# The low half of the weight split, on VectorE in place of GpSimd, in a hybrid decoder layer

## The chip, the cores and the metric

One core of one Trainium2 chip runs the whole program. The metric is the device time of one execution in microseconds (us). Engines are named as the profile names them: PE is TensorE, ACT is ScalarE, DVE is VectorE, POOL is GpSimd, SP is the engine that issues most transfers.

## What is computed

One layer over 512 tokens of width 1024, all in float32. Three token mixers run side by side on one combined projection, are gated and summed, and a feed-forward follows (from the reference, cut):

```
h = rms_norm(x, norm1_g)
u = h @ w_in
y_a = dsa_mixer(...)   # 16 heads; an index picks the 128 keys that count
y_b = nsa_mixer(...)   # 16 heads; compressed blocks, chosen blocks, window
y_c = ssd_mixer(...)   # Mamba-2, chunks of 128 tokens, 32 heads
mix = gates[0]*(y_a @ w_br_dsa) + gates[1]*(y_b @ w_br_nsa) + gates[2]*(y_c @ w_br_ssd)
x = x + mix @ w_out
h = rms_norm(x, norm2_g)
x = x + square(relu(h @ w_ff1)) @ w_ff2
```

## The kernel before, in words

**Split products.** A float32 operand is written as hi + lo, both in a faster float32 format (F32R). A large product is then three matmuls: hi with hi, hi with lo, lo with hi (`mm3`, L317 to L319). The weights are split as they arrive. `WS.load` (L130) sends 128x1024 weights from memory into one of three `wraw` buffers by SP. `WS.split` (L141) makes `whi`, a rounding copy on ScalarE (L150), and `wlo`, the subtraction `wraw - whi` (L151); each has six buffers. `tick` keeps the splits up to three pieces ahead of the products, and `free` gives the buffers back once the last product that reads them is issued. There are 212 pieces in a run.

**Two streams.** `filler` (L543 on) yields all large products: projections of `h`, then the branch products (`branches`, L1200), `w_out` and the feed-forward (`ff_up`, L1338, `ff_down`, L1367). `main` yields what comes between: the DSA index (L709), DSA attention, the SSD (L1071), NSA attention. The loop at the end takes steps from both in turn by estimated costs. Main's instructions have a higher priority. A scheduler of the framework then sets the order on each engine by priority and by its own reckoning of when an operand is ready; each engine works through its order strictly. So a change of one instruction's engine can move instructions on every engine.

**Attention** (`pipeline`, L820) takes a unit of 4 heads and 128 queries: scores on TensorE (L755, L756), mask and maximum on VectorE (L757), exponential on ScalarE (L764), scaling of `p` on VectorE for three heads (L777) and on GpSimd for the fourth (L775), transposes on TensorE (L791), hi and lo of the transposed `p` on ScalarE and VectorE (L795, L796), products with V (L803, L804; L943 for the compressed branch), the sum `yt` (L810, L811), written to memory as rows of y and read back as `yr` (L664) for the branch products.

**SSD** (`stage2`, L1094 on): VectorE makes `E` from the cumulated decays (eight L1102 for a chunk and group, then L1110) and `cbm` (L1100); GpSimd scales `xs` three times (L1105, L1108, L1112) and the state (L1132); TensorE multiplies (L1098, L1121, L1127, L1137). Beside it runs the convolution of the filler, on VectorE (L684).

**Branch products and feed-forward.** `branches` takes a0, a1, c0, c1, b0, b1 in order; b1 can't begin until the last NSA rows are back from memory. In `ff_up` ScalarE applies relu (L1362), VectorE squares (L1363), ScalarE rounds (L1364), VectorE takes the low half (L1365).

Of the kernel before, what the change touches and what calls it, by code (L numbers as in the profile page):

```python
# [10 lines left out]
ALU = mybir.AluOpType  # L11
# [25 lines left out]
def build_kernel(ctx, tc, A, out):  # L37
    nc = tc.nc
    pe, act, dve, pool = nc.tensor, nc.scalar, nc.vector, nc.gpsimd
    done = set()  # L40

    def dram(ap, off, dims):
        return bass.AP(tensor=ap.tensor, offset=ap.offset + off, ap=dims)

    def bc(ap, shape):
        return ap.to_broadcast(shape)

    def f(ap):
        return ap.bitcast(F32)
# [3 lines left out]
    def popen(name, side="left", space=None, bufs=1):  # L53
        kw = dict(name=name, bufs=bufs, side=side)
        if space is not None:
            kw["space"] = space
            kw.pop("side")
        cm = tc.tile_pool(**kw)
        p = cm.__enter__()
        open_pools[name] = cm  # L60
        return p
# [17 lines left out]
    yc_d = scratch("yc_d", [2048, S])  # L79
    rs_d = scratch("rs_d", [4, 128])  # L80

    # ------------------------------------------------------------------ constants
    cp = popen("const")
    psp = ctx.enter_context(tc.tile_pool(name="psp", bufs=1, space=PSUM))

# [31 lines left out]
    g1b = x0.tile([128, D], F32, name="g1b")  # L117
    act.dma_start(g1b, dram(A["norm1_g"], 0, [[0, 128], [1, D]]))

    # ------------------------------------------------------------------ weights  # L120
    class WS:
        def __init__(s):
            s.specs, s.raw, s.hl = [], {}, {}
# [17 lines left out]
        def split(s):  # L141
            i = s.nsplit
            while s.nload <= i:
                s.load()
            _, n, w = s.specs[i]
            r = s.raw.pop(i)
            m = n * w
            hi = wp.tile([128, 1024], F32R, name="whi", tag="whi", bufs=NS)
            lo = wp.tile([128, 1024], F32R, name="wlo", tag="wlo", bufs=NS)
            act.activation(hi[:, :m], r[:, :m], AF.Copy)  # L150
            pool.tensor_tensor(lo[:, :m], r[:, :m], f(hi[:, :m]), op=ALU.subtract)  # L151
            s.hl[i] = (hi[:, :m].rearrange("p (a b) -> p a b", b=w), lo[:, :m].rearrange("p (a b) -> p a b", b=w))
            s.nsplit += 1

# [70 lines left out]
            ff1[q + 1] = plan_ff1(q + 1)  # L225
        ff2[q] = plan_ff2(q)

    # first weights run ahead of the activations
    for t in range(1, NB):
        ws.load()  # L230
        nc.sync.dma_start(xt[t], dram(A["x"], t * 128 * D, [[D, 128], [1, D]]))

    # ------------------------------------------------------------------ small constants
    def bcast_load(name, ap, n, pl):
        t = pl.tile([128, n], F32, name=name)
        nc.sync.dma_start(t, dram(ap, 0, [[0, 128], [1, n]]))
        return t
# [24 lines left out]
                           pattern=pat or [[step, n]], channel_multiplier=chm)  # L262
        return t

    # ------------------------------------------------------------------ x -> h^T
    sq_junk = x0.tile([128, D], mybir.dt.bfloat16, name="sq_junk")
    ss1 = cp.tile([128, NB], F32, name="ss1")
    rs1 = cp.tile([128, NB], F32, name="rs1")
# [18 lines left out]
    for i, b in enumerate((2, 3)):  # L287
        for half in range(2):
            cur = 2 * b + half
            r = slice(64 * half, 64 * half + 64)  # L290
# [21 lines left out]
    dve.tensor_copy(pos2[64:128], pv_[:, :, :, 1])  # L312
    pclose("x0")

    # ------------------------------------------------------------------ matmul helpers
    def mm3(o, lh, ll, rh, rl, first, last):
        pe.matmul(o, lh, rh, start=first, stop=False)  # L317
        pe.matmul(o, lh, rl, start=False, stop=False)  # L318
        pe.matmul(o, ll, rh, start=False, stop=last)  # L319
# [43 lines left out]
    hh = lambda k: hTh[:, k, :]  # L363
    hl = lambda k: hTl[:, k, :]

    # ------------------------------------------------------------------ persistent attention operands
    def r_tile(pl, name, shape):
        return pl.tile(shape, F32R, name=name)

# [5 lines left out]
    kc = r_tile(kv, "kc", [128, 2, 2, 32])  # L375
# [74 lines left out]

    RB, AB, TB, EB, TG = [int(v) for v in "33222"]

    # ------------------------------------------------------------------ filler: all large products
    def q_block(o, plan):
        ss = stg.tile([128, NB, 8], F32, name="ssq", bufs=2)

# [25 lines left out]


    def cmp_prep(u1, e1):
        """k_cmp and v_cmp operands from the raw kc, vc columns."""
        for v in range(2):
            xc = e1.tile([128, 16, 2, 32], F32, name="xc", bufs=1)
            wh = []
            for i in range(2):
                w_ = e1.tile([128, 8, 64], F32, name="cmpw", tag="cw", bufs=2)  # L490
                nc.sync.dma_start(w_, dram(A["nsa_cmp_w"], v * 131072 + i * 65536, [[64, 128], [8192, 8], [1, 64]]))
                wh.append(w_)
            pool.memset(xc[:, :, :, 31:32], 0.0)
            p = ps("pT", [128, S])
            for t in range(NB):
                pe.transpose(p[:, t * 128:t * 128 + 128], u1[:, t, v * 128:v * 128 + 128], ident)
            yield 440
            for g in range(2):
                for half in range(2):
                    r = slice(64 * half, 64 * half + 64)  # L500
                    base = p[64 * g:64 * g + 64, half:half + 1]
                    win = bass.AP(tensor=base.tensor, offset=base.offset, ap=[base.ap[0], [2, 16], [16, 31]])
                    dve.tensor_tensor(xc[r, :, g, :31], win, bc(pos2[r, v, :, None], [64, 16, 31]), op=ALU.add)
            yield 440
            pc = ps("pT", [128, 512])
            for a in range(16):
                pe.matmul(pc[:64, :64], xc[:, a].rearrange("p g n -> p (g n)"), wh[a // 8][:, a % 8], start=a == 0, stop=a == 15)
            if v == 0:
                kx = e1.tile([64, 64], F32, name="kx")
                dve.tensor_copy(kx, pc[:64, :64])  # L510
                yield 1800
                rt = rms_rows(e1, kx[:, None, :], 64, 1, 1.0 / 64, EPS)
                dve.scalar_tensor_tensor(kx, kx, rt[:64, 0:1], g_nsa[:64, 0, :], op0=ALU.mult, op1=ALU.mult)
                kcs = e1.tile([64, 2, 2, 64], F32R, name="kcs")
                kxb = bc(kx[:, None, :], [64, 2, 64])
                act.activation(kcs[:, 0], kxb, AF.Copy)
                dve.tensor_tensor(kcs[:, 1], kxb, f(kcs[:, 0]), op=ALU.subtract)
                for i in range(2):
                    pk = ps("pT", [128, 64], F32R)
                    pe.transpose(pk, kcs[:, i].rearrange("p a b -> p (a b)"), identr[:64, :64])  # L520
                    act.activation(kc[:, :, i], f(pk).rearrange("p (g n) -> p g n", g=2), AF.Copy)
                yield 600
            else:
                vx = e1.tile([64, 64], F32, name="vx")
                dve.tensor_copy(vx, pc[:64, :64])
                yield 1800
                sel = e1.tile([64, 2, 4, 32], F32, name="sel")
                dve.tensor_copy(sel, bc(ident[:64, 0:64].rearrange("p (g n) -> p g n", g=2)[:, :, None, :], [64, 2, 4, 32]))
                zero = e1.tile([128, 256], F32, name="zero")
                pool.memset(zero, 0.0)  # L530
                vzf = vz.rearrange("p a b c d -> p (a b c d)")
                for z in range(2):
                    act.activation(vzf[:, 256 * z:256 * z + 256], zero, AF.Copy)
                for g in range(2):
                    pk = ps("pT", [128, 64])
                    pe.matmul(pk, sel[:, g].rearrange("p a b -> p (a b)"), vx, start=True, stop=True)
                    for h in range(4):
                        r = slice(32 * h, 32 * h + 32)
                        act.activation(vz[r, g, h % 2, 0], pk[r], AF.Copy)
                        dve.tensor_tensor(vz[r, g, h % 2, 1], pk[r], f(vz[r, g, h % 2, 0]), op=ALU.subtract)  # L540
                    yield 300
# [130 lines left out]

    ypools = {}

    # ------------------------------------------------------------------ conv + silu of the SSD inputs
    def conv(m, p):
        cw = lambda k: convc[:, k * 24 + m:k * 24 + m + 1]
        raw = stg.tile([128, S], F32, name="craw", tag="r", bufs=RB)
# [23 lines left out]
                nc.sync.dma_start(dst.rearrange("(t p) c -> p t c", p=128), ev)  # L702
            defer(1, tr)

    # ------------------------------------------------------------------ DSA index and its top 128
    MASK = {}
    RIDX = R0

# [27 lines left out]
        pclose("idx")  # L736
        return sv

    # ------------------------------------------------------------------ attention units
    class U:  # L740
        pass

# [120 lines left out]
            u.prep = lambda i=i: prep(i)  # L863
        return us

    # ------------------------------------------------------------------ NSA
    SM = {}
    PC = {}
    CT = {}

    def cmp_a(b, g, q2, ratio):
        """Compressed-branch softmax of 8 heads and the block choice."""
        s_ = ps("sc", [128, 512])
        sv = s_.rearrange("p (h i n) -> p h i n", i=2, n=32)
        for h in range(8):
# [136 lines left out]
                    us.append(u)  # L1012
        return us

    # ------------------------------------------------------------------ SSD
    def ssd_prelude():
        n = [128, 128]
        pre = [gp.tile([128, 4, 128], F32, name="pre", tag="gt", bufs=TG) for _ in range(2)]
# [177 lines left out]
        a = t[r0:r0 + n, :]  # L1196
        return bass.AP(tensor=a.tensor, offset=a.offset, ap=[[0, 128]] + [list(e) for e in a.ap])

    # ------------------------------------------------------------------ branches, merge, w_out, feed-forward
    def branches(ya):  # L1200
        bp = popen("br")
        mix = bp.tile([128, KT, S], F32, name="mixf")
# [89 lines left out]
        pclose("yC")  # L1292
        pclose("yB")
        pclose("br")
        # w_out + residual + norm2
        fp = popen("ff")
        x2 = fp.tile([128, NB, D], F32, name="x2")
        h2h = fp.tile([128, KT, S], F32R, name="h2h")
# [82 lines left out]
        pclose("ffl")  # L1381
        pclose("ff")

    # ------------------------------------------------------------------ the two streams and their merge
    def main():
        nonlocal at
        HI[0] = 0
# [32 lines left out]
    while True:  # L1420
        with tc.high_priority(offset=HI[0]):
            r = next(mg, None)
# [42 lines left out]
```

## Time and profile before

| | |
|---|---|
| runs, median (lowest to highest of 3) | 1495.65 us (1494.98 to 1497.01) |
| profiled execution, first to last instruction | 1496.3 us |
| PE busy | 1400.1 us |
| DVE busy | 1013.8 us |
| POOL busy | 715.6 us |
| ACT busy | 691.0 us |

The profiled execution is one of the program's runs, taken with a hardware profiler; its span stands for its own time and lies within the three runs shown. A row of a group of instructions reads: line, engine, operation, what it writes and reads, shape, how often; then busy time, mean duration in ns, and the engine's idle time just before them with what ended it. A duration runs from the start of an instruction to its end, with any time in which it is held after it has started. Matmul records overlap, so their mean is longer than the distance between them.

### The profile page before, as it was taken

The page shows a single profiled execution, that of the slowest core. Times are in us where ns is not written, and L with a number is a line of the kernel's source. Part 1 is how long each engine was busy: PE and PEld are TensorE (multiplying, and loading weights), DVE is VectorE, ACT ScalarE, POOL GpSimd, SP SyncE. Part 2 cuts the span into 40 slices and gives each one's busy share as a digit, 9 for nine tenths or more (in the row PEclk, how much of TensorE's full clock was granted, in tenths as well). Part 3 has the DMA queues.
Part 4 walks back from the last instruction along what each step waited for, and adds up shares of the span by engine and source line. Part 5 has one row for each costly group of instructions (what it writes and reads, how often), then busy time and mean ns, then how long its engine had stood idle before and what let it go on. Part 6 is the DMA issues. An engine that isn't in the chain of part 4 may idle for free.

```text
span 1496.3 us, 19760 instructions
## 1 busy us (share of the span) xinstructions
PE 1400.1 (94%) x6832; PEld 1149.9 (77%) x6832; DVE 1013.8 (68%) x1887; ACT 691.0 (46%) x1364; POOL 715.6 (48%) x456
## 2 busy tenths in 40 slices
PE   6998999899988898899999999999999999999999
PEld 5886788677866676787788877777678888888887
DVE  4699956789789987757767898786645751433411
ACT  4545445667644454545555555545333441422220
POOL 5544534434245366544334765644753542544351
PEclk9999999999999998999999999999999999999999
DMA  5323464443565565654324744422652322323231
GB/s 194 99 77 106 150 203 130 125 122 94 139 198 173 166 199 159 200 170 130 106 89 147 206 140 117 117 78 78 211 201 82 113 99 71 127 73 112 83 106 50
DMA packets 218272, 195.92 MB, mean 131 GB/s; under 512 B 15664, under 2 KB 165564, under 8 KB 218172
## 3 DMA queue, kind: packets, MB, share of 16 engines
q1 hardware_dynamic: 212700, 183.12, 41.3%
q0 software_dynamic: 4608, 8.39, 2.0%
q10 hardware_dynamic: 864, 3.15, 0.5%
q8 instruction: 54, 0.88, 0.2%
q14 instruction: 46, 0.38, 0.1%
HBM read 157.85 MB, written 36.77 MB: 130 GB/s over the span
## 4 chain that ended last, share of the span: by engine, by line
PE 56%; DVE 29%; ACT 5%; DMA 5%; issue 4%; POOL 2%; SPq 0%; DVEq 0%; ACTq 0%; POOLq 0%
PE pj L318 15%; PE pj L319 15%; PE pj L317 15%; DVE E L1102 3%; DVE cacc L684 3%; DVE p L777 3%; ACT p L764 3%; DVE ptl L796 2%; DVE mask L731 2%; DVE m L730 1%; DVE p L757 1%; PE pT L791 1%; PE sc L1137 1%; PE sc L755 1%; DMA wraw<-in_w_in_dram 1%
## 5 line engine op out<-in xcount | busy, mean ns | idle before, releaser
L151 POOL TENSOR_TENSOR wlo<-wraw,whi 128x1024 fp32r<-128x1024 f32 (+3 forms) x212 | 479.0, 2269 | 416.7 <-ACT whi L150 394.9
L150 ACT ACTIVATE whi<-wraw 128x1024 fp32r<-128x1024 f32 (+3 forms) x212 | 207.3, 982 | 210.9 <-PE pj L319 102.1
L319 PE MATMUL pj<-hTh,wlo 128*128 128x512 f32 x384 | 156.8, 408 | 0.0
L317 PE MATMUL pj<-hTh,whi 128*128 128x512 f32 x384 | 155.4, 405 | 0.1
L318 PE MATMUL pj<-hTl,whi 128*128 128x512 f32 x384 | 154.8, 403 | 0.0
L764 ACT ACTIVATE p<-p,nb,rs 128x256 f32<-128x256 f32 (+3 forms) x192 | 123.3, 644 | 59.2 <-DVE nb L762 58.9
L317 PE MATMUL pj<-whi,hTh 128*128 128x512 f32 (+2 forms) x352 | 138.7, 396 | 8.1 <-DVE zo L575 2.2
L318 PE MATMUL pj<-wlo,hTh 128*128 128x512 f32 (+2 forms) x352 | 138.7, 395 | 0.8 <-POOL wlo L151 0.8
L319 PE MATMUL pj<-whi,hTl 128*128 128x512 f32 (+2 forms) x352 | 139.0, 396 | 0.0
L1363 DVE TENSOR_TENSOR fr<-fr 128x512 f32<-128x512 f32 x32 | 80.8, 2530 | 56.2 <-ACT fr L1362 56.2
L1371 DVE TENSOR_TENSOR x<-x,pj 128x512 f32<-128x512 f32 x32 | 22.0, 687 | 138.3 <-PE pj L319 137.8
L777 DVE TENSOR_SCALAR p<-p,rc 128x256 f32<-128x256 f32 (+3 forms) x144 | 113.3, 837 | 1.1
L775 POOL TENSOR_TENSOR p<-p,rc 128x256 f32<-128x256 f32 (+3 forms) x48 | 37.9, 790 | 152.5 <-DVE rc L770 51.8
L317 PE MATMUL pj<-yh,whi 128*128 128x512 f32 x256 | 103.4, 406 | 5.1 <-DVE gld L1282 3.1
L318 PE MATMUL pj<-yl,whi 128*128 128x512 f32 x256 | 103.6, 405 | 0.2 <-DVE yl L666 0.2
L319 PE MATMUL pj<-yh,wlo 128*128 128x512 f32 x256 | 103.0, 402 | 0.0
L318 PE MATMUL pj<-wlo,fh 128*128 128x512 f32 x256 | 99.6, 389 | 0.0
L319 PE MATMUL pj<-whi,fo 128*128 128x512 f32 x256 | 99.6, 389 | 0.0
L317 PE MATMUL pj<-whi,fh 128*128 128x512 f32 x256 | 98.8, 389 | 0.0
L319 PE MATMUL pj<-h2h,wlo 128*128 128x512 f32 (+1 forms) x256 | 96.2, 376 | 0.0
L318 PE MATMUL pj<-h2l,whi 128*128 128x512 f32 (+1 forms) x256 | 96.2, 376 | 0.0
L317 PE MATMUL pj<-h2h,whi 128*128 128x512 f32 (+1 forms) x256 | 96.1, 376 | 0.0
(333 smaller groups left out, 3322.5 us busy)
## 6 DMA issues: line engine op xcount, KB each, us to landing
wraw<-in_w_in_dram SPq DMA_DIRECT2D x84, 512.0 KB, 4.1
wraw<-in_w_ff_dram SPq DMA_DIRECT2D x64, 512.0 KB, 4.0
gld<-g_d SPq DMA_DIRECT2D x48, 256.0 KB, 3.1
q_d<-qev SPq DMA_DIRECT2D x32, 256.0 KB, 2.3
qu<-q_d POOLq DMA_DIRECT2D x32, 256.0 KB, 4.2
E<-ac_d SPq DMA_DIRECT2D x16, 512.0 KB, 4.3
wraw<-in_w_br_ssd_dram SPq DMA_DIRECT2D x16, 512.0 KB, 4.2
g_d<-gth SPq DMA_DIRECT2D x24, 256.0 KB, 2.0
```

Source lines behind the costliest of these rows:

```text
L150: act.activation(hi[:, :m], r[:, :m], AF.Copy)
L151: pool.tensor_tensor(lo[:, :m], r[:, :m], f(hi[:, :m]), op=ALU.subtract)
L317: pe.matmul(o, lh, rh, start=first, stop=False)
L318: pe.matmul(o, lh, rl, start=False, stop=False)
L319: pe.matmul(o, ll, rh, start=False, stop=last)
L684: dve.scalar_tensor_tensor(acc[:, sh:], raw[:, :S - sh], cw(k), acc[:, sh:], op0=ALU.mult, op1=ALU.add)
L731: dve.match_replace(wk, m8, wk, TAKEN)
L764: act.activation(u.p[h][:, :n], u.p[h][:, :n], AF.Exp, bias=u.nb[:, h:h + 1], scale=rs8[:, u.b, u.h0 + h:u.h0 + h + 1], accum_out=u.sm[:, ...
L775: pool.tensor_tensor(u.p[h][:, :n], u.p[h][:, :n], bc(rc[:, h:h + 1], [128, n]), op=ALU.mult)
L777: dve.tensor_scalar(u.p[h][:, :n], u.p[h][:, :n], rc[:, h:h + 1], None, op0=ALU.mult)
L1102: dve.tensor_scalar(u.E[:, h], u.E[:, h], col(sv["acm"], c, g)[:, h:h + 1], 0.0, op0=ALU.subtract, op1=ALU.min)
L1363: dve.tensor_tensor(r, r, r, op=ALU.mult)
```

## The change

One line. The subtraction that makes the low half of a weight piece is issued on VectorE.

```
@@ def split(s)
             act.activation(hi[:, :m], r[:, :m], AF.Copy)
-            pool.tensor_tensor(lo[:, :m], r[:, :m], f(hi[:, :m]), op=ALU.subtract)
+            dve.tensor_tensor(lo[:, :m], r[:, :m], f(hi[:, :m]), op=ALU.subtract)
```

The rest of the diff takes out comments. The scheduler's order changes on every engine. Two places:

VectorE, where the SSD begins. `E` and `cbm` belong to the SSD, `cacc` and `craw` to the convolution, `wlo` is the moved subtraction. Before:

```order
L1102 TENSOR_SCALAR E<-E,sv_acm 128x128 x8
L684 SCALAR_TENSOR_TENSOR cacc<-craw,convc,cacc 128x509
L684 SCALAR_TENSOR_TENSOR cacc<-craw,convc,cacc 128x510
L684 SCALAR_TENSOR_TENSOR cacc<-craw,convc,cacc 128x511
L1102 TENSOR_SCALAR E<-E,sv_acm 128x128 x8
```

And of the change:

```order
L151 TENSOR_TENSOR wlo<-wraw,whi 128x1024
L1102 TENSOR_SCALAR E<-E,sv_acm 128x128 x8
L684 SCALAR_TENSOR_TENSOR cacc<-craw,convc,cacc 128x509
L684 SCALAR_TENSOR_TENSOR cacc<-craw,convc,cacc 128x510
L684 SCALAR_TENSOR_TENSOR cacc<-craw,convc,cacc 128x511
L1102 TENSOR_SCALAR E<-E,sv_acm 128x128 x8
L151 TENSOR_TENSOR wlo<-wraw,whi 128x1024
```

The subtractions now stand on VectorE, in line with the SSD's work and the convolution's; before, they stood on GpSimd.

TensorE, at the end of NSA attention. `yh` and `yl` are halves of y (branch products, the filler), `pv` the product of `p` with V, `vz` the values of the compressed branch. Before, the last rows:

```order
L317 MATMUL pj<-yh,whi 128x512
L318 MATMUL pj<-yl,whi 128x512
L319 MATMUL pj<-yh,wlo 128x512
L803 MATMUL pv<-pth,v_s_314 128x512
L804 MATMUL pv<-ptl,v_s_314 128x512
L317 MATMUL pj<-yh,whi 128x512
L318 MATMUL pj<-yl,whi 128x512
```

And of the change:

```order
L791 MATMUL pF<-ident,p 128x128 x4
L791 MATMUL pT<-ident,p 128x128 x4
L943 MATMUL pv<-cph,vz 128x128 x4
L803 MATMUL pv<-pth,v_w_316 128x512
L804 MATMUL pv<-ptl,v_w_316 128x512
L803 MATMUL pv<-pth,v_s_314 128x512
L804 MATMUL pv<-ptl,v_s_314 128x512
L943 MATMUL pv<-cph,vz 128x128 x4
```

In the change the last 98 matmuls of the attention (17 each of L755 and L756, 32 of L791, 20 of L803 and L804, 12 of L943) stand with no branch product between them; before there were branch products among them, and 24 more of b0 behind them. In the change those products stand earlier.

## Rows read from the trace of the kernel before

**Rows 1.** The page: busy time of each engine, its share, its instructions.

```profile
PE 1400.1 (94%) x6832; PEld 1149.9 (77%) x6832; DVE 1013.8 (68%) x1887; ACT 691.0 (46%) x1364; POOL 715.6 (48%) x456
```

**Rows 2.** By stretch: length, each engine's busy time (x instructions), granted clock, DMA share, GB/s.

```profile
50.00:250.00 200.00, 186.91 (x953) 154.96 (x952) 160.94 (x389) 95.67 (x210) 93.26 (x58) 0.98 0.45 133
...
250.00:410.00 160.00, 150.09 (x752) 122.98 (x751) 134.63 (x255) 106.87 (x216) 60.40 (x38) 0.99 0.44 116
...
410.00:640.00 230.00, 197.05 (x951) 155.32 (x951) 194.23 (x309) 110.01 (x222) 125.25 (x81) 0.91 0.63 183
...
640.00:1010.00 370.00, 357.50 (x1799) 294.88 (x1798) 286.21 (x634) 196.61 (x423) 191.51 (x137) 0.99 0.44 129
...
1010.00:1150.00 140.00, 130.72 (x631) 105.62 (x630) 88.34 (x151) 57.51 (x118) 77.22 (x53) 0.99 0.49 152
...
1150.00:1450.00 300.00, 300.00 (x1389) 251.25 (x1388) 120.66 (x90) 94.30 (x121) 128.70 (x54) 1.00 0.29 92
```

**Rows 3.** TensorE's waits: who, for whom, us in total, times, longest.

```profile
PE pT L1127 <- DVE cbm L1100: 14.1, 3, 7.1
...
PE pT L791 <- DVE p L777: 11.4, 11, 2.1
...
PE pT L1150 <- DVE hst L1133: 6.8, 3, 4.1
```

**Rows 4.** Timelines of VectorE and GpSimd in DSA attention, VectorE in SSD: start, us.

```profile
267.27 5.22 DVE L777 TENSOR_SCALAR p<-p,rc 128x512 f32<-128x512 f32 x2
...
267.31 7.41 POOL L151 TENSOR_TENSOR wlo<-wraw,whi 128x1024 fp32r<-128x1024 f32 x3 [0.24 <-ACT whi L150]
...
556.92 9.30 DVE L1102 TENSOR_SCALAR E<-E,sv_acm 128x128 f32<-128x128 f32 x8
```

**Rows 5.** VectorE's groups; for two, shortest/median/longest ns.

```profile
L777 DVE TENSOR_SCALAR p<-p,rc 128x256 f32<-128x256 f32 (+3 forms) x144 | 113.3, 837 | 1.1
...
L777 DVE TENSOR_SCALAR p<-p,rc x144: 274/486/2720, 211.7 to 1051.7; 128x256 f32<-128x256 f32 x36, 128x512 f32<-128x512 f32 x36, 128x128 f32<-128x128 f32 x36, 128x384 f32<-128x384 f32 x36
...
L1102 DVE TENSOR_SCALAR E<-E,sv_acm 128x128 f32<-128x128 f32 x128 | 61.7, 552 | 7.4 <-DMA E<-ac_d 7.3
...
L1102 DVE TENSOR_SCALAR E<-E,sv_acm x128: 272/278/2431, 417.4 to 615.9; 128x128 f32<-128x128 f32 x128
...
L1363 DVE TENSOR_TENSOR fr<-fr 128x512 f32<-128x512 f32 x32 | 80.8, 2530 | 56.2 <-ACT fr L1362 56.2
```

**Rows 6.** Groups by shape: the subtraction, and like instructions of VectorE.

```profile
L151 POOL TENSOR_TENSOR wlo<-wraw,whi 128x1024 fp32r<-128x1024 f32 x172 | 420.8, 2456 | 382.4 <-ACT whi L150 360.7 <-DVE rc L772 14.0 <-DMA wraw<-in_w_in_dram 4.1
...
L151 POOL TENSOR_TENSOR wlo<-wraw,whi 128x512 fp32r<-128x512 f32 x32 | 42.4, 1333 | 20.9 <-ACT whi L150 20.9
...
L1110 DVE TENSOR_TENSOR E<-E,cbm 128x1024 f32<-128x1024 f32 x16 | 23.1, 1443 | 1.4 <-ACT E L1103 1.1
...
L1110 DVE TENSOR_TENSOR E<-E,cbm x16: 1210/1224/3404, 431.9 to 620.0; 128x1024 f32<-128x1024 f32 x16
...
L1365 DVE TENSOR_TENSOR fo<-fr,fh 128x512 fp32r<-128x512 f32 x32 | 22.1, 692 | 19.8 <-ACT fh L1364 19.6
```

**Rows 7.** The subtraction alone, GpSimd, by stretch.

```profile
50.00:1010.00 960.00, 263.65 (x116) 0.97 0.49 141
```

**Rows 8.** Groups by shape in attention, VectorE and ScalarE.

```profile
L757 DVE CUSTOM_DVE_ANT_0 p<-sc,caus 128x128 f32<-128x128 f32 x48 | 13.2, 281 | 7.8 <-PE sc L756 7.7
...
L796 DVE TENSOR_TENSOR ptl<-pT,pth 128x512 fp32r<-128x512 f32 x95 | 64.2, 681 | 3.6 <-ACT pth L795 3.4
...
L764 ACT ACTIVATE p<-p,nb,rs 128x128 f32<-128x128 f32 x48 | 23.1, 482 | 12.3 <-DVE nb L762 12.2
...
L795 ACT ACTIVATE pth<-pT 128x512 fp32r<-128x512 f32 x95 | 54.9, 591 | 40.3 <-PE pT L791 39.3 <-PE pv L803 0.6
```

**Rows 9.** The chain that ended last, 1055 to 1080 us: start, us, what.

```profile
1062.61 3.48 DMA yb_d<-yt
...
1066.19 3.20 DMA yr<-yb_d
```

## The prediction

> **What bounds the kernel now.** I read the busy shares first, then the table by stretch, then what TensorE waits for, and last the timelines of VectorE and GpSimd around those waits. TensorE is busy 1400.1 of 1496.3 us, so 96.2 us at most is idle to be won back without changing its work [rows 1]. Subtracting its busy time from each stretch [rows 2] gives: 13.1 us idle from 50 to 250 us (the index), 9.9 from 250 to 410 (DSA attention), 33.0 from 410 to 640 (SSD), 12.5 from 640 to 1010 (NSA attention), 9.3 from 1010 to 1150, and none from 1150 to 1450 (feed-forward, 300.00 of 300). The rest lies in the load of x and the end. So 68.5 us from 50 to 1010 is open to this change, and the feed-forward can gain nothing, whatever VectorE does there.
>
> Whom does TensorE wait for there? For VectorE: the longest rows are cbm (14.1 us), p of L777 (11.4) and hst (6.8) [rows 3]. VectorE is not full: 776 of 960 us from 50 to 1010 (160.94 + 134.63 + 194.23 + 286.21) [rows 2]. Its single instructions are late. At 267 us two scalings of p take 5.22 us together while GpSimd runs three subtractions without a break [rows 4]; the median of L777 is 486 ns [rows 5]. The same shape difference is plainest in the feed-forward: L1363 and L1365 are both 128x512 with two operands in SBUF, one right after the other, yet L1363 takes 2530 ns and L1365 692 [rows 5, 6]; the first starts while a GpSimd subtraction of 2456 ns is under way. So here a VectorE instruction that meets a GpSimd one is held until that one is about done.
>
> **The change, part by part.** *Taken from GpSimd:* 212 subtractions, 172 of them 128x1024 at 2456 ns (420.8 us) and 32 of 128x512 at 1333 (42.4) [rows 6]. GpSimd falls from 715.6 [rows 1] to about 237 us; nothing on it is a bound, so this by itself is worth nothing. What stood behind them in its order (the fourth head of p, the q loads, the powers) comes earlier. No DMA moves to another queue.
>
> *Added to VectorE:* the same 212. The nearest rows are L1110 (128x1024, two operands in SBUF, median 1224 ns) and L1365 (128x512, 692) [rows 6]. I take 1.22 and 0.69 us: 172 x 1.22 + 32 x 0.69 = 232, and about 8 for the eight odd shapes: 240 us. The mean of L1110 is 1443, because some meet GpSimd; with that the large ones would cost 38 us more. These are the ends, and I take the lower one, since two thirds of GpSimd's work is gone. The Trainium skill, "SBUF — State Buffer", section "Who interferes with whom", has a rule that speaks against the change: a VectorE instruction with two SBUF inputs, which the new subtraction is, itself contends with a GpSimd instruction that reads SBUF. The stretched L1110 agrees; by the rule alone the sum for VectorE would be the 38 us higher one.
>
> *Given back to VectorE:* L1363 falls to the 0.69 of L1365, 32 x 1.84 = 59 us, all in the feed-forward. L777: 144 x (837 - 486) = 51 us; L1102: 128 x (552 - 278) = 35 us [rows 5]. Of the last two I count two thirds (57 us), the share of the subtractions in GpSimd's busy time (479 of 716). Smaller groups are left out, which makes this a floor. From 50 to 1010, where 116 subtractions lie [rows 7], VectorE so gets at most 116 x 1.22 = 142 and gives back at least 57: 776 + 85 = 861 of 960 us, 90%. It gets fuller, but it does not run full.
>
> *TensorE's stalls, 50 to 1010.* A low-priority subtraction in front of an attention instruction now holds it 1.2 us at most, not 2.5, and it is placed there by the order rather than met by chance. In the SSD eight L1102 in a row took 9.30 us [rows 4] where eight medians are 2.2 [rows 5], and cbm, for which TensorE waited, stood behind them. Bounds: none of the 68.5 us goes (VectorE fuller), or all. I take, by stretch: index 13 to 8 (VectorE 80% full and its long chain of maxima has one SBUF operand, so little changes), DSA 10 to 3, SSD 33 to 15 (GpSimd's own SSD products stay and still hold L1102), NSA 12 to 6. Sum: -36 us.
>
> *What is late next.* The order of the change puts the attention stream later against the large products on TensorE. At its end 98 attention matmuls stand with no product between them; before, products stood among them up to the last two. So the cover is gone there, and the stretch goes at the pace of VectorE and ScalarE. On VectorE: 17 score reductions of mostly 281 ns (4.8 us), 15 scalings at no more than the 486 of [rows 5] (7.3), 8 low halves of 681 (5.4), and some 4 for sums and small ones: about 21 us [rows 8]. On ScalarE 20 exponentials at 482 and 8 copies at 591: 15 us [rows 8]. VectorE is the longer, and with some 4 us for the last unit's chain the stretch takes 25 us. TensorE's work in it I estimate at 12: 20 products with V are 512 wide, at 1389 large ones in 300 us or 0.22 each [rows 2] 4.4 us; the other 78 are a quarter to half as wide, at half the time 8. Idle: 13 us. Then the last rows of y must go out and come back (3.48 and 3.20 us [rows 9], and about 1 for their split) with 12 products, 2.7 us, to cover it: 5 us. Together 18. Of the 9.3 us idle from 1010 to 1150 before I set 5 against this place, the rest against the second norm: **+13 us**. Ends: +4, if the units overlap fully; +30, if the six units go one after another, at some 7 us each by the same durations.
>
> Start and end I leave as they are. The sum: 1496.3 - 36 + 13 = 1473. The profiled span lies 0.65 us over the median of the three runs, 1495.65; I forecast **1473**, and 1460 to 1487 for this case, from stalls won back between 24 and 50.
>
> **The rivals.** *VectorE stands at the subtraction (slower).* VectorE works in order. On GpSimd the subtraction waited 360.7 us for ScalarE's copy [rows 6], and this held nobody. On VectorE whatever follows is held too. For: ScalarE's copies wait in turn for buffers of TensorE. Against: the order knows the copy's place, and half of that wait lies in the feed-forward. Price: if each of the 116 subtractions from 50 to 1010 stands 0.6 us too early, VectorE loses 70 us and, at half of it on TensorE, 35; the gain of 36 is eaten and the bare end stays: 1496 - 36 + 35 + 13 = 1508. It decides from about 0.4 us per subtraction: 46 us of VectorE, 23 of TensorE, which is all that the sum above leaves. The Trainium skill, "Perfetto Trace Analysis", section "Optimizing Scalar/DVE Operations", points the same way: a saturated VectorE may be relieved by GpSimd, which this change undoes; but it adds that the two share a port, so that this might not help, and the 2530 ns above bear out the second half.
>
> *The two terms cancel.* The stalls won back are only as many as the bare end costs, 13 to 18 us: 1491 to 1500. For it: the index stretch is VectorE's own chain, and GpSimd's SSD products stay.
>
> *More comes back.* In the SSD the granted clock is 0.91 [rows 2], between the levels of 1.2 and 2.4 GHz, after stretches at 0.98 and 0.99 with fewer gaps; at 0.91 of 230 us some 20 us of work are lost. If the gaps go and half of that with them, and more than 36 of the stalls, the time is 1440 to 1460. Against: the SSD's matmuls are small and unevenly spaced for reasons of their own.
>
> **Chances.** The forecast 0.48, more comes back 0.14, the two cancel 0.15, VectorE stands 0.23. A measurement of this kernel can tell 0.2%, 3 us, from no change. Two thirds of the cancelling case lie within that (0.10), the rest counts half to each side with a little more to the faster: faster 0.65, same 0.10, slower 0.25. The range takes the forecast, most of the case below it, the cancelling case and the near half of the slower: 1450 to 1507.
>
> **What would show it.** Right: L1363 near 0.69 us, L777's mean near its median, the new subtraction near 1.22 us, VectorE's total within 100 us of the 1013.8 before, TensorE's idle time from 410 to 640 about halved, and a new hole of 15 to 20 us at the end of NSA. Wrong: L1363 still at 2.5 us (GpSimd was not the cause), or waits of VectorE at the subtraction for ScalarE that add up to over 50 us before the feed-forward.

## The result, and the profile after

The change takes 1456.72 us (median of 4 runs, 1452.96 to 1458.86) against 1495.32 for the kernel before beside it (4 runs): a ratio of 0.9739, 95% interval 0.9721 to 0.9757, so 38.6 us or 2.6% less. The forecast of 1473 erred by 16 us, on the side of too small a gain; the range of 1450 to 1507 held the time.

The page of the changed kernel, its busy times (compare [rows 1]):

```profile
PE 1396.3 (96%) x6832; PEld 1151.8 (79%) x6832; DVE 1020.5 (70%) x2099; ACT 692.6 (48%) x1364; POOL 259.8 (18%) x244
```

Its span is 1457.2 us, 39.1 less than before. TensorE's idle time fell from 96.2 to 60.9 us, and its busy time by 3.8: 35.3 + 3.8 = 39.1. GpSimd lost 456 us; VectorE, which took over 248 us of subtractions, is only 6.7 us busier than before.

The table by stretch, columns as in [rows 2]:

```profile
0.00:50.00 50.00, 37.69 (x177) 31.34 (x178) 29.08 (x67) 26.66 (x55) 7.36 (x22) 0.97 0.54 174
...
410.00:640.00 230.00, 214.33 (x1064) 170.99 (x1063) 186.09 (x339) 112.50 (x227) 85.64 (x67) 0.96 0.69 209
640.00:1010.00 370.00, 357.00 (x1801) 295.74 (x1799) 294.64 (x729) 199.43 (x445) 120.74 (x100) 0.98 0.43 124
...
1110.00:1410.00 300.00, 300.00 (x1392) 251.32 (x1392) 124.32 (x144) 94.95 (x121) 0.00 (x0) 1.00 0.30 93
```

TensorE's idle time in the SSD stretch (410 to 640) is 230 - 214.33 = 15.7 us, half of the 33.0 before, while VectorE is busy for 186 us of it, 8 less than before. A second profile of the same kernel (span 1458.2 us, from its run among the experiments) has 20.0 there, and 66.7 us of idle time in all in place of 60.9; so a term of this section can differ by some 5 us from one execution to the next. NSA is 13.0, hardly different from 12.5. The feed-forward was full and is full. The two stretches that aren't shown have 193.53 busy of 200 (50 to 250) and 160.00 of 160 (250 to 410).

VectorE's groups (compare [rows 5, 6]):

```profile
L151 DVE TENSOR_TENSOR wlo<-wraw,whi 128x1024 fp32r<-128x1024 f32 (+3 forms) x212 | 248.1, 1173 | 124.9 <-ACT whi L150 122.7
...
L777 DVE TENSOR_SCALAR p<-p,rc 128x256 f32<-128x256 f32 (+3 forms) x144 | 68.2, 522 | 0.8
...
L684 DVE SCALAR_TENSOR_TENSOR cacc<-craw,convc,cacc 128x509 f32<-128x509 f32 (+2 forms) x72 | 54.8, 761 | 0.7
...
L1102 DVE TENSOR_SCALAR E<-E,sv_acm 128x128 f32<-128x128 f32 x128 | 46.4, 433 | 12.6 <-DMA E<-ac_d 12.6
...
L1363 DVE TENSOR_TENSOR fr<-fr 128x512 f32<-128x512 f32 x32 | 21.9, 685 | 0.0
```

L1363 went from 2530 ns to 685, L777 from 837 to 522 (its median is 419 here). L1102 is at 433, still far above its median (281 ns here), since GpSimd's own SSD products are still there. VectorE stood 122.7 us at the subtraction for ScalarE's copy, but 87 of those us lie between 1110 and 1410, in the feed-forward. From 50 to 1010 it is this:

```profile
L151 DVE TENSOR_TENSOR wlo<-wraw,whi 128x1024 fp32r<-128x1024 f32 (+2 forms) x128 | 147.9, 1158 | 25.9 <-ACT whi L150 25.7
```

TensorE's waits (compare [rows 3]):

```profile
PE pT L1098 <- DMA bcx<-BC_d: 7.6, 5, 2.0
PE sc L755 <- DVE mx L757: 4.8, 6, 1.6
...
PE pT L791 <- DVE p L777: 2.7, 4, 1.3
...
PE pT L1150 <- DVE hst L1133: 1.3, 1, 1.3
...
PE pT L1098 <- DVE cbm L1100: 0.7, 1, 0.7
```

The wait for cbm, 14.1 us before, is down to 0.7, that for p from 11.4 to 2.7, that for hst from 6.8 to 1.3. What is longest now in the SSD stage is a transfer.

The end of NSA, the place of the forecast hole, by stretch:

```profile
1000.00:1010.00 10.00, 9.96 (x41) 8.93 (x40) 6.36 (x38) 7.24 (x27) 1.01 (x2) 0.50 0.17 60
1010.00:1025.00 15.00, 10.93 (x35) 7.53 (x34) 8.68 (x27) 7.34 (x22) 1.22 (x3) 0.61 0.08 18
1025.00:1035.00 10.00, 6.44 (x19) 4.15 (x18) 3.36 (x5) 3.12 (x5) 0.00 (x0) 0.65 0.37 120
```

The hole is there, but only 7.7 us of these 35 show as idle. In the first row TensorE is busy for 9.96 of 10 us and yet the granted clock is 0.50: the lower of the two levels, 1.2 GHz, and 41 matmuls go by. In the 5 us before 998 us, where the clock falls, it was busy for 3.04 at 0.99.

### The profile page after: what moved, and what is told of

It is laid out like the page before. It is cut to its first block, busy times and chain, and to the rows that moved or that the text cites. A ratio compares the mean times of both kernels' runs of the same rounds, so it can differ in the third digit from the quotient of the medians.

```text
span 1457.2 us, 19734 instructions
## 1 busy us (share of the span) xinstructions
PE 1396.3 (96%) x6832; PEld 1151.8 (79%) x6832; DVE 1020.5 (70%) x2099; ACT 692.6 (48%) x1364; POOL 259.8 (18%) x244
## 4 chain that ended last, share of the span: by engine, by line
PE 63%; DVE 18%; DMA 9%; issue 4%; ACT 3%; POOL 1%; SPq 0%; DVEq 0%; ACTq 0%; POOLq 0%
PE pj L317 18%; PE pj L318 17%; PE pj L319 17%; DVE wlo L151 3%; DMA gld<-g_d 3%; DVE E L1102 2%; PE pT L791 2%; DMA E<-ac_d 1%; ACT p L764 1%; PE sc L756 1%; PE sc L755 1%; DVE p L777 1%; DMA wraw<-in_w_in_dram 1%; DVE ptl L796 1%; DVE p L757 1%
## 5 line engine op out<-in xcount | busy, mean ns | idle before, releaser
L151 DVE TENSOR_TENSOR wlo<-wraw,whi 128x1024 fp32r<-128x1024 f32 (+3 forms) x212 | 248.1, 1173 | 124.9 <-ACT whi L150 122.7
L319 PE MATMUL pj<-h2h,wlo 128*128 128x512 f32 (+1 forms) x256 | 96.2, 376 | 0.0
L319 PEld LDWEIGHTS pj<-hTh,wlo 128*128 128x128 f32 x384 | 72.8, 190 | 15.5 <-issue 1.5
L318 PEld LDWEIGHTS pj<-hTl,whi 128*128 128x128 f32 x384 | 72.8, 190 | 15.5 <-issue 2.0
L317 PEld LDWEIGHTS pj<-hTh,whi 128*128 128x128 f32 x384 | 72.7, 189 | 14.7 <-issue 1.4
```

Of the source, the lines that this page charges most:

```text
L151: dve.tensor_tensor(lo[:, :m], r[:, :m], f(hi[:, :m]), op=ALU.subtract)
```

## The experiments

Theory: a GpSimd instruction that reads SBUF holds VectorE's instructions that need the same access, and the change wins by taking those reads away before the feed-forward. Rivals: GpSimd's queue was full, or the new order of the work did it; and, for the size, other prices of the forecast's single terms. Ratios are to the kernel before, with 95% intervals; ratios a few thousandths apart can be told from each other only where the intervals part.

**Only the feed-forward's pieces on VectorE.** `ff1[0][0]` is the number of its first piece.

```
-            pool.tensor_tensor(lo[:, :m], ...
+            (dve if i >= ff1[0][0] else pool).tensor_tensor(lo[:, :m], ...
```

> Only the 64 pieces of the feed-forward weights are subtracted on VectorE, the other 148 on GpSimd as before. Theory (stalls of VectorE behind GpSimd's subtraction cost TensorE time, in the stages where TensorE waits): L1363 falls from 2530 to about 690 ns, VectorE loses some 59 us and gains 78, and the time stays within 4 us of before (1491 to 1499), since TensorE never waits there. Rival (a less held VectorE is worth time wherever it is): faster by 10 us or more.

Measured: 1495.03 us, ratio 0.9996 [0.9977, 1.0015]. L1363 falls to 685 ns as in the change, and nothing comes of it: 59 us of VectorE returned where TensorE has no idle time.

**All but the feed-forward's.** The same line with the two engines exchanged.

> The opposite: 148 pieces on VectorE, the 64 of the feed-forward on GpSimd. Theory: within 4 us of the change, 1453 to 1461, with L1363 back at 2500 ns. Rival (the feed-forward carries part of the gain): 1465 or more.

Measured: 1462.61 us, ratio 0.9772 [0.9735, 0.9810], against 0.9739 [0.9721, 0.9757] for the change: 1.6 us above the theory's range and below the rival's, with intervals that overlap. L1363 is still slow:

```profile
L1363 DVE TENSOR_TENSOR fr<-fr 128x512 f32<-128x512 f32 x32 | 78.7, 2462 | 58.5 <-ACT fr L1362 58.5
```

So the gain lies before the feed-forward, and the most striking row of the profile was worth nothing.

**GpSimd reads the same again.** The change, and then GpSimd subtracts the same pieces over the raw weights, which nobody reads any more.

```
             dve.tensor_tensor(lo[:, :m], r[:, :m], f(hi[:, :m]), op=ALU.subtract)
+            pool.tensor_tensor(r[:, :m], r[:, :m], f(hi[:, :m]), op=ALU.subtract)
```

> The change, and GpSimd does each subtraction once more, into the raw piece that nobody reads afterwards: 212 x 2.4 us of GpSimd reading SBUF come back, beside VectorE's own subtraction. Theory (the lock): L777 and L1102 go back to means over 700 and 480 ns, VectorE's total over 1150 us, TensorE's idle time from 50 to 650 us from 22 back to over 45, and the time to 1490 to 1530. Rival order (the scheduler's new order made the gain): 1455 to 1470. Rival queue (what stood behind the subtraction in GpSimd's order made the gain): as the theory, about 1490.

Measured: 1601.76 us, ratio 1.0705 [1.0672, 1.0738]. The gain is gone, but the time is 70 us above the theory's upper end, and L777 comes to 617 ns where over 700 was expected (L1102 to 522, as expected). The page's row of busy times and two stretches:

```profile
PE 1447.0 (90%) x6832; PEld 1171.3 (73%) x6832; DVE 1273.6 (80%) x2099; ACT 690.7 (43%) x1364; POOL 779.9 (49%) x456
```

```profile
50.00:250.00 200.00, 169.36 (x803) 138.13 (x802) 183.47 (x351) 75.23 (x162) 86.36 (x47) 0.91 0.37 109
...
410.00:640.00 230.00, 200.52 (x975) 156.41 (x974) 214.47 (x338) 122.51 (x247) 117.10 (x70) 0.96 0.54 156
```

VectorE now has the subtractions and the holds too: 253 us more than in the change, 92 to 93% busy in these stretches. It is nearly full there, which the expectation had not priced. The convolution's L684 (L685 in this kernel), which reads two large operands, shows the hold by itself (shortest/median/longest ns):

```profile
L685 DVE SCALAR_TENSOR_TENSOR cacc<-craw,convc,cacc x72: 722/750/2960, 300.5 to 524.9; 128x509 f32<-128x509 f32 x24, 128x510 f32<-128x510 f32 x24, 128x511 f32<-128x511 f32 x24
```

In the trace 26 of the 72 begin while a subtraction of GpSimd is under way, and these take 2086 ns in the mean; the 30 that meet none take 743.

**GpSimd as busy, without reading.** The change, and two `memset` over each raw piece.

```
             dve.tensor_tensor(lo[:, :m], r[:, :m], f(hi[:, :m]), op=ALU.subtract)
+            for _ in range(2):
+                pool.memset(r[:, :m], 0.0)
```

> The change, and GpSimd fills each raw piece twice with zeros after the split (about 2.1 us for a large one): GpSimd is as busy as before the change and its queue as full, but it reads no SBUF. Theory (held by GpSimd's reads): two-operand instructions of VectorE (L684, L1363) stay at their short durations, and the time stays within 12 us of the change, 1455 to 1469. Rival queue: about as the run with the second subtraction, 1485 or more. Rival order: 1455 to 1470 too, so this run tells queue from the other two, and the run before tells order from lock.

Measured: 1461.99 us, ratio 0.9770 [0.9739, 0.9801]. GpSimd is busy for 621 us with 668 instructions, 361 us more than in the change, and the gain is there within the interval. Rows of this kernel (its lines stand two further down; L1365 is L1363 of the change, L1104 its L1102, L686 its L684):

```profile
L153 POOL MEMSET wraw<- 128x1024 f32 (+3 forms) x424 | 372.1, 886 | 514.3 <-DVE wlo L151 502.3 <-DVE ss L273 2.2
...
L1104 DVE TENSOR_SCALAR E<-E,sv_acm 128x128 f32<-128x128 f32 x128 | 53.6, 514 | 10.0 <-DMA E<-ac_d 9.8
...
L1365 DVE TENSOR_TENSOR fr<-fr 128x512 f32<-128x512 f32 x32 | 21.9, 685 | 0.0
...
L686 DVE SCALAR_TENSOR_TENSOR cacc<-craw,convc,cacc x72: 729/741/924, 255.4 to 459.9; 128x509 f32<-128x509 f32 x24, 128x510 f32<-128x510 f32 x24, 128x511 f32<-128x511 f32 x24
```

Instructions with two operands in SBUF aren't held by a write: 33 of the 72 on L686 begin while a `memset` is under way, and none of these takes over 753 ns. (L1365 alone would be weak evidence: of its 32 only one begins under a `memset`, and takes 686.) The one-operand L1102 and L777 are held by writes where they meet them: four of L1102 begin under a `memset` with nothing else of GpSimd beside them and take 463 to 809 ns, where 282 is usual; seven of L777 do, and take up to 757. Most of the step from 433 to 514 in its mean comes from GpSimd's own SSD products, which 61 of the 128 meet here and 45 in the change. And L796, which reads one operand from TensorE's output and one in SBUF, is held by neither: before the change 37 of its 120 begin while GpSimd is at work, and none takes over 692 ns.

The queue rival falls: GpSimd's queue is long here too, and the gain stays. Order was held fixed in no run, since each edit moves the scheduler's order on every engine. The gain is there under the change's order and under the different one of this kernel, which makes it unlikely that one lucky order carries it; more isn't shown.

This is the rule of the Trainium skill, "SBUF — State Buffer", section "Who interferes with whom": a two-input VectorE instruction contends with a GpSimd instruction that reads SBUF, not with one that only writes. The 753 ns here at most and the 2960 one run above agree.

**The hole.** The trace shows the hole; is its price the run of 98? Two kernels keep the first pieces of the weight stream on GpSimd, which also changes the order at the end of NSA; the change was run beside them.

```
+            (pool if i < 28 else dve).tensor_tensor(lo[:, :m], ...
```

> The change itself once more, as the measure for the three kernels beside it. Every theory: 1453 to 1461 us, about 2.6% under the kernel before.

> The change, but the first 28 pieces of the weight stream (taken up to about 160 us, while VectorE is busy for 0.85 of the time) are still subtracted on GpSimd; the pieces after them go to VectorE. In this order of work the run of 98 attention matmuls without a product between them, at about 1000 to 1030 us of the change, is gone: the last products still lie between them. Theory (the bare run costs what it cost in the change's trace, about 18 to 20 us of idle time and lowered clock together; the first 28 pieces give up at most the 2.5 us of idle time that the change saved before 50 us and about half of the 6.6 it saved from 50 to 250 us): 14 us or so less than the change, 1438 to 1449 us, and no stretch of 0.5 to 0.6 granted clock after 990 us. Rival (the bare run is paid anyway: the matmuls wait for VectorE and ScalarE in the attention wherever the products lie, and the first 28 pieces hold VectorE up again): 1455 to 1468 us, and the idle time from 50 to 410 us goes back to over 15 us.

> As the run with 28 pieces, with the first 36 (up to about 210 us). Theory: the bare run is gone as well; about 2 us more of the idle time from 50 to 250 us comes back, so 1439 to 1452 us, not faster than with 28 by more than 2 us. Rival (GpSimd is the better place for the whole index stage, since VectorE's MAX8 and MATCH_REPLACE8 there are not held by GpSimd's reads): faster than with 28 by 3 us or more.

Measured: the change 1456.92 us, 0.9738 [0.9718, 0.9758]; with 28 pieces 1469.96, 0.9827 [0.9809, 0.9845]; with 36 pieces 1461.89, 0.9764 [0.9741, 0.9786]. The theory missed for both kernels, and a stretch at the lower clock is there all the same (0.50 from 1028 to 1040 us with 28 pieces). The rivals did no better: the time with 28 pieces is 2 us above its rival's range too, with 12.7 us idle from 50 to 410 where over 15 was said. With 36 it is 8 us faster than with 28, as its rival had it, but not for its reason: the index stage, 50 to 250 us, is idle for 12.7 us in one and 12.6 in the other. The 100 us around the end of the attention, in the kernel with 28 pieces, and below it in the change of the first profile and of the second:

```profile
965.00:1065.00 100.00, 82.95 (x377) 64.65 (x376) 70.09 (x173) 47.04 (x113) 25.16 (x24) 0.91 0.40 122
```

```profile
955.00:1055.00 100.00, 86.90 (x384) 68.90 (x383) 76.73 (x198) 52.44 (x125) 24.86 (x22) 0.85 0.39 119
```

```profile
955.00:1055.00 100.00, 84.90 (x408) 66.64 (x407) 78.43 (x205) 54.24 (x129) 27.09 (x24) 0.91 0.40 121
```

And in the kernel before:

```profile
993.00:1093.00 100.00, 92.67 (x436) 73.24 (x435) 72.06 (x151) 46.44 (x107) 55.90 (x45) 0.98 0.45 137
```

Without the run of 98 the hole is as large: 17.0 us idle at a clock of 0.91, against 13.1 at 0.85 and 15.1 at 0.91 in the two profiles of the change, and 7.3 at 0.98 before. So it isn't priced by the length of that run. Part of it has moved: TensorE waits 7.6 us in all for the halves of y with 28 pieces and 8.4 with 36, 3.6 and 2.7 in the two profiles of the change, 0.9 before. What sets the whole stays open: in the kernel before, 24 products still stood behind the last attention tile, and no run changed that alone.

The run of 98 itself, up to the first product behind it, in the two profiles of the change:

```profile
993.00:1028.00 35.00, 26.27 (x100) 20.29 (x98) 22.65 (x88) 19.41 (x60) 4.11 (x7) 0.62 0.20 60
```

```profile
998.00:1029.00 31.00, 20.14 (x99) 14.41 (x97) 22.09 (x88) 19.11 (x60) 4.12 (x7) 0.83 0.22 65
```

The 13 us by which the kernel with 28 pieces is slower come mostly from the start: its idle time to 250 us is 15.2 + 12.7 = 27.9 us, in the change 12.3 + 6.5 = 18.8. The forecast had 5 us for this, and nothing before 50 us. VectorE's chain of maxima was rightly taken for immune (L730 takes 556 ns before and 558 in the change); it is two-operand instructions beside it that got shorter (L725 from 850 to 609 ns). With 36 pieces the idle time to 250 us is 26.4, hardly less, and yet the time lies within the change's interval, with 5 us less idle time from 640 to 1010; so what the 9 us are worth at the end isn't settled.

**What GpSimd still reads in NSA.** `SPL` names the engine of yl (L666), L1285 adds the branches, and L775 scales the fourth head of p.

```
-SPL = {"a0": 1, "a1": 1, "c0": 1, "c1": 1, "b0": 1, "b1": 0}
+SPL = {"a0": 0, "a1": 0, "c0": 0, "c1": 0, "b0": 0, "b1": 0}
-            if h == 3:
+            if h == 4:
-                (dve if br == "b1" else pool).tensor_tensor(mix[:, m], ...
+                dve.tensor_tensor(mix[:, m], ...
```

> The change, and with it the two other streams of two-operand work that GpSimd still has in the NSA stage (640 to 1025 us): the products that lie between p and rc for the fourth head, and the adds of the branches' mix. Theory 1 (what is left of the idle time of TensorE in that stage, 13.0 us from 640 to 1010, is VectorE held by these two on GpSimd): it falls to 8 or less and the time to 1446 to 1453 us; the one-operand operation on p falls from 0.52 to under 0.40 us in the mean. Theory 2 (VectorE has 295 of 370 us filled there, and 50 to 60 instructions more put it on the path): 1457 to 1475 us, with more waits for p than the change has. The bare run of attention matmuls at the end is 110 long in either.

Measured: 1439.99 us, ratio 0.9625 [0.9609, 0.9641], 17 us below the change and more than expected (the first theory's sign is there: the operation on p takes 380 ns in the mean). From 640 to 940 us TensorE was busy for 292.15 us in the change; here:

```profile
640.00:940.00 300.00, 298.62 (x1541) 250.03 (x1540) 250.74 (x662) 168.01 (x363) 6.50 (x12) 1.00 0.45 132
```

Its parts alone:

> Of the run with both NSA streams on VectorE (1440 us) only the adds of the branches' mix go there (32 of 128x512, 1.6 us each on GpSimd, which also takes the products' low half yl with the one order of the two engines); the products of p and rc for the fourth head stay on GpSimd. Theory 1 (each stream holds VectorE in proportion to its time on GpSimd: about 92 us of mix and yl, 38 us of p): some two thirds of the 17 us, 1444 to 1449 us. Theory 2 (the products p lie in the chain that TensorE waits for, the mix does not): 1451 to 1457 us.

> The other part alone: the products of p and rc for the fourth head on VectorE (48 of up to 128x512, 0.79 us each on GpSimd, about 0.4 us in VectorE's one-operand form), mix and yl stay on GpSimd. Theory 1: a third of the 17 us, 1450 to 1453 us. Theory 2: 1440 to 1447 us.

Measured: the mix and yl alone 1441.01 us, 0.9627 [0.9613, 0.9640]; p alone 1457.37, 0.9724 [0.9705, 0.9744]. Neither theory: the mix and yl give all of it, p nothing. From 640 to 940 us TensorE's idle time, 7.9 us in the change, is 1.1 with the mix and yl alone and 8.3 with p alone. The adds in the change (shortest/median/longest ns, first and last start), and VectorE's wait for a gate (us, times, longest):

```profile
L1285 POOL TENSOR_TENSOR mixf<-mixf,gld x32: 1261/1568/2283, 776.7 to 994.7; 128x512 f32<-128x512 f32 x32
```

```profile
DVE gld L1272 <- DMA gld<-g_d: 16.7, 10, 4.5
```

That wait in the kernel with the mix alone:

```profile
DVE gld L1272 <- DMA gld<-g_d: 1.3, 3, 0.8
```

The adds' median on GpSimd was 1295 ns before and is 1568 now: VectorE's new two-operand subtractions hold GpSimd in their turn. In the trace 15 of the 32 begin under such a subtraction and take 1902 ns in the mean; the 7 that meet none take 1327. Each add also keeps a gate buffer, and the next gate's load waits for it: 5.6 us of VectorE's time before, 16.7 in the change. That wait is no measure of the time by itself: with the `memset`s it is 7.1 us at 1462 us. How much of the 16 us is this, how much the holds and how much yl, no run separates.

**The same move without the change.**

> The kernel before (the subtraction on GpSimd), with the mix adds and yl on VectorE alone, as in the run with the mix only. Theory 1 (the change itself made the mix chain late: GpSimd's adds went from a median of 1295 to 1568 ns when the large subtraction came to VectorE, and VectorE's wait for the gate loads behind them from 5.7 to 16.7 us): without the change there is little to win, 1489 to 1497 us. Theory 2 (the mix on GpSimd costs its 16 us wherever the subtraction stands): 1476 to 1484 us.

Measured: 1517.59 us, ratio 1.0129 [1.0106, 1.0152]. Both theories missed: it costs 1.3%. There the adds on VectorE meet the subtractions on GpSimd:

```profile
L1285 DVE TENSOR_TENSOR mixf<-mixf,gld x40: 659/690/2880, 844.5 to 1116.7; 128x512 f32<-128x512 f32 x40
```

The median is 690 ns, the longest 2880; 18 of the 40 meet a subtraction. But in good part the loss is of another kind. TensorE's wait for the halves of y, before and in this kernel:

```profile
PE pj L317 <- ACT yh L665: 0.9, 1, 0.9
```

```profile
PE pj L317 <- ACT yh L665: 12.7, 5, 8.8
```

The 8.8 us stand at the end of NSA, where the new order leaves no product behind the last attention tile to cover the way of y through memory. TensorE's idle time grew by 17 us in all, from 96.2 to 113.1. The four kernels together: subtraction and mix on GpSimd 1495, subtraction alone moved 1457, mix alone moved 1518, both moved 1441. What a move is worth hangs on what stands beside it; how much of that is GpSimd's reads and how much the order of the work, these four don't separate.

**The SSD's products too.** In addition to both NSA streams, L1105, L1108, L1112 and L1132 on VectorE (`pool.` to `dve.` in each).

> Both NSA streams and the four products of the SSD stage (52 of 128x512, 1.1 to 1.4 us each on GpSimd, 65 us in all) on VectorE, so that GpSimd reads next to nothing any more. Theory 1 (what is left of the waits of that stage is VectorE held by GpSimd): the 128 subtractions on E (0.437 us in the mean) come to 0.28 us, which gives back 20 us, against 52 x 0.69 = 36 us added; VectorE is then at about 202 of 230 us there, TensorE waits less for E and the time is 1430 to 1438 us. Theory 2 (VectorE, filled to 0.8 there, has no room for 36 us more): more waits for E, cbm and hst, 1441 to 1455 us.

Measured: 1434.24 us, ratio 0.9580 [0.9565, 0.9595], as the first theory had it, and the fastest of all: its interval lies below that of both NSA streams alone (0.9609 to 0.9641).

```profile
L1102 DVE TENSOR_SCALAR E<-E,sv_acm x128: 273/282/291, 422.0 to 583.0; 128x128 f32<-128x128 f32 x128
```

With GpSimd reading next to nothing there (65 us busy in the whole run), no L1102 is longer than 291 ns; in the kernel before the longest was 2431 [rows 5]. VectorE, at 198 of 230 us, wasn't too full.

## Why the prediction was right, and where it was off

- **The mechanism** held at the places named: L1363 at 685 ns, the new subtraction at a median of 1222, VectorE's total 6.7 us above before, the SSD's idle time about halved (15.7 and 20.0 us in two profiles), a hole at the end of NSA, though not one of 15 to 20 us. L777's mean, 522 ns, came only part of the way to its median. The runs with reading and writing GpSimd show for two-operand instructions that it is the reads.
- **"Added 240 us"** came to 248.1. Of the two ends, the lower price (1.22) was right, not the 38 us higher one: only 26 of the 212 begin while GpSimd is at work, and 12 of these take over 1300 ns, up to 2311. The rule of the Trainium skill, "SBUF — State Buffer", section "Who interferes with whom", by which two-input instructions contend with GpSimd's reads, holds for those all the same.
- **"Given back at least 59 + 57"** was a floor and far below the truth: VectorE is 6.7 us busier after taking 248.1, so 241 came back. L1363 gave 58.9, L777 45.1 and L1102 15.3, where two thirds of 51 and 35 were forecast; L684, not counted, gave 20.1, and the other 100 came in groups of under 12 us each. So "861 of 960 us" of VectorE from 50 to 1010 became 796.
- **TensorE's stalls, "-36"**, by stretch: index -6.6 (forecast -5), DSA -9.9 (-7), SSD -17.3 (-18; by the second profile -13.0). To these come -2.5 before 50 us, which the sum left at zero. NSA is the step that failed: +0.5 from 640 to 1010 us and +0.5 behind it, 1 in all, where -6 for stalls and +13 for the hole made +7.
- **"+13 for the hole"** was right on its place and wrong on its nature. The run of 98 up to the first product takes 35.0 and 31.0 us in the two profiles, not far from the 25 and the wait for y that were forecast. What was mis-sized is TensorE's own work in it: 12 us forecast, 26.3 and 20.1 measured, so that 8.7 and 10.9 us are idle where 18 were forecast. By the 100 us rows above the hole cost 13.1 - 7.3 = 5.8 us of idle time or, by the second profile, 7.8, and a granted clock of 0.85 or 0.91 in place of 0.98 besides, which a row of busy time doesn't show. Nor is its price set by the 98 bare matmuls, as the kernels with 28 and 36 pieces show.
- **"NSA 12 to 6"** didn't come: outside the hole the mix on GpSimd got slower and its buffers later. The runs without it there have the 7.9 us down to 1.1 (yl moved with it). The prediction had not counted anyone waiting for GpSimd's mix.
- **Busy time -3.8**: the sum had none. The clock in the SSD stretch rose from 0.91 to 0.96, which the rival "more comes back" named; the lower clock in the hole took part of that. In the second profile busy time is 8.6 below before, so this term too differs between executions.
- These add up: -2.5 in the start, -1.6 and -2.9 more in index and DSA, +0.7 in the SSD, -6 in NSA and its end, -3.8 of busy time: -16.1 us, the distance between the sum's 1473.3 and the profiled 1457.2. It is the sum of one execution, and partly terms that cancel. In the forecast's own range the upper end of 1487 goes with 22 us won back, not 24.
- **VectorE stands at the subtraction** was the rival on the other side. It decides from 46 us between 50 and 1010; the row says 25.7, and TensorE's wait for p fell rather than grew. That half of the wait is harmless in the feed-forward was right as well (87 of 122.7 us).

## What to carry to other kernels

A VectorE instruction with two operands in SBUF that is much longer than its like beside a GpSimd instruction that reads SBUF was held here, and its cost is to be read in the stage where somebody waits for it: here 59 us of held time in the feed-forward were worth nothing, and 15 us in the SSD were among those that counted. Try two-operand work off GpSimd all together, not only piece by piece: here one move made 2.6%, another by itself lost 1.3% (in good part to a new order at the end of NSA), and all of them made 4.2%. When pricing a stretch in which TensorE goes idle, look at its granted clock as well as at its idle time, in more than one profile.

## What was not expected of the hardware

TensorE at the lower clock level while almost wholly busy: 0.50 over 10 us with 9.96 us busy, 41 matmuls of the attention and no branch product among them. In the second profile the same part of the run of 98, with the same gaps before it (3.06 of 5 us busy, 3.04 in the first), ran at 1.00:

```profile
1005.00:1015.00 10.00, 7.61 (x47) 5.76 (x46) 9.26 (x51) 9.30 (x34) 1.43 (x3) 1.00 0.17 59
```

So the same stretch shows as lowered clock in one execution and as idle time in the other, and the run of 98 is 4 us longer in the first. Busy time may hide stalls too, since matmul records overlap: from 250 to 410 us there were 752 matmuls in 150.09 us before [rows 2], 830 in 160.00 after: 10% more matmuls for 6.6% more busy time. The shapes there were not counted apart, so this part is a hint only.

The hold works both ways. GpSimd's adds went from a median of 1295 to 1568 ns when VectorE got more two-operand work, and when both engines did all subtractions VectorE alone grew by 253 us and the time by 145. The Trainium skill, "Perfetto Trace Analysis", section "Optimizing Scalar/DVE Operations", says that shifting work between these two might not help. The 1517.59 us fit that, though a good part of that loss is the wait for y; 1434.24 us show that the three streams together on VectorE do help.
